# V rows that begin inside the query steps of a PEER stage, with query sums and V sums in different PSUM banks

## The chip, the cores and the metric

The kernel runs on one core of a Trainium2 chip. The metric is the device time of one execution in microseconds (us); less is better. Three runs of the kernel before gave 3059.07 to 3061.05 us, with a median of 3060.49 us.

The core has five engines that run their own instruction queues in order: TensorE (PE in the profile; its weight loads are PEld), VectorE (DVE), ScalarE (ACT), GpSimd (POOL) and SyncE (SP). They wait for each other by semaphores. Transfers between device memory and on-chip memory go over 16 DMA engines; here SP issues the weight loads and POOL issues the gathers.

## The reference

The model is two blocks of layers on 256 tokens of width 2048. The change touches only the last stage, a PEER layer: product keys choose 16 of 16384 experts for each of 8 heads and each token; each chosen expert has a row of `u` and a row of `v`.

```
def peer(x, wq, keys1, keys2, u, v):
    q = (xf @ wq).reshape(t, PEER_HEADS, PEER_QDIM)
    s1 = jnp.einsum('thd,kd->thk', q[..., :half], keys1)
    s2 = jnp.einsum('thd,kd->thk', q[..., half:], keys2)
    ...
    expert = jnp.take_along_axis(cand_i, pos, axis=-1).reshape(t, -1)
    gate = jax.nn.softmax(top_s.astype(jnp.float32), axis=-1)
    ...
        z = jnp.einsum('cd,ced->ce', xc, u[ec])
        act = jax.nn.gelu(z, approximate=False) * gc
        return jnp.einsum('ce,ced->cd', act, v[ec])
```

For each token 8 x 16 rows of `u` are dotted with the token, and 8 x 16 rows of `v` are summed with the weights that come out. Then the result is added to the stream and normalised.

## The kernel before

All tensors of 256 tokens are held as two token tiles of 128 (`TT` = 2). Everything ahead of the last stage is a long list of matmul steps that `run` works through. A step takes one weight tile of 512 KB: `load` brings two such tiles in one transfer of 1 MB, ACT makes a rounded copy `hi` (`split_hi`, L102), DVE the remainder `lo` (`split_lo`, L86), and PE multiplies with both. `run` splits `LOOK_SPLIT` = 3 steps ahead. There are 4 buffers for `lo`, so the split of a step can start only when PE has done the step 4 before it.

The last 32 steps are the queries of the 8 heads: 4 steps a head, built by `unit_B2`, each of 24 matmuls (L417 to L419) that add into one PSUM tile of the head. Here they are called step 0 to step 31, and the heads 0 to 7, so that steps 4h to 4h+3 belong to head h. After a head's fourth step, `e_query` scales the sum (DVE, `eq<-eq,stE_R`, called the query sum's read below), multiplies with the keys (PE, `esc`, L1291), copies the scores (ACT, `es`), and `e_route` finds the 16 experts by a row of small DVE instructions. Head 0 to 7 of token tile 0 are routed first, then those of token tile 1.

A gather (`gather`, L1379, issued by POOL) fetches for each of the 128 tokens of a tile one row of `e_u` or `e_v`: 128 x 2048 x 4 bytes, or 1.049 MB. The text counts these as rows: 256 U rows and 256 V rows, 16 of each for every head and token tile. A U row is worked on by one DVE instruction of 2048 columns (L1410). A V row is worked on by PE: ACT makes a diagonal matrix (`dg`), and four fp32 matmuls of 512 columns (L1428) add the row into `vacc`, which takes 4 PSUM banks; the profile shows 8 matmuls for these. Only some rows of the last two heads are added on DVE.

`e_stream` sets the order of gathers and row work. It is a generator that `run` advances once after every step (`pump`): it issues gathers as long as a row buffer is free, takes the oldest pending row, emits its work, puts the buffer back, and yields. There are 3 row buffers during the query steps. When the last head's scores are copied, `wide_rows` adds 6 more, made of the weight buffers and the token tiles that the queries no longer need; their names begin with `rows_w` and `rows_x`. A V row is allowed (`v_ok`) only after all 8 heads have their scores (`Ee["q"] == EH`) and when its head's U rows are all done; while both kinds are allowed they alternate.

PSUM has two kinds of tiles of two banks each, two of either: `acc_tile` and `side_tile`. Before, a head's query sum takes an `acc_tile`, its scores a `side_tile`, and the V sums of token tile 0 take both `acc_tile`s once the queries are through.

Line numbers are those of the kernel before, unless the text says that they are of the changed kernel (there the V matmuls are L1443, the U instruction L1425, the gather L1394).

Of the kernel before, what the change touches and what calls it, by code (L numbers as in the profile page):

```python
# [22 lines left out]
T = 256  # L23
# [39 lines left out]
def tile_model(ctx: ExitStack, tc: tile.TileContext, x, xT, par, a_in, a_out, kv_in, kv_f, b_in, b_out,  # L63
# [12 lines left out]
    def acc_tile(name):  # L76
        return psum.tile([P, 2, 512], F32, tag="acc", bufs=2, name=name)

    def side_tile(name):
        return psum.tile([P, 2, 512], F32, tag="side", bufs=2, name=name)  # L80

    def w4(name, shape=(P, 1024), dt=F32):
        return work.tile(list(shape), dt, tag="w4", bufs=NW4, name=name)

    def tt_(o, a, b, op):
        V.tensor_tensor(o, a, b, op=op)  # L86

    def mul(o, a, b):
        V.tensor_tensor(o, a, b, op=OP.mult)
# [7 lines left out]
    def stt(o, a, s, b, op0, op1):  # L97
        V.scalar_tensor_tensor(o, a, s, b, op0=op0, op1=op1)  # L98

    def act(o, i, f, bias=0.0, scale=1.0, accum=None):  # L100
        if accum is None:
            S.activation(o, i, f, bias=bias, scale=scale)  # L102
        else:
            S.activation(o, i, f, bias=bias, scale=scale, accum_out=accum)  # L104
# [4 lines left out]
    def spawn(gen):  # L109
        tasks.append(gen)  # L110
# [232 lines left out]
    def resid_norm(st, chunks_ready, xt, wn):  # L343

        for c in range(4):
            while chunks_ready[0] <= c:
                yield
            yield from x_to_T(c, xt, wn)
            norm_chunk(st, c)
        yield  # L350
        yield from norm_end(st)
# [47 lines left out]
        steps[-1].post = lambda: spawn(cb(box["acc"].rearrange("p a (b t) -> p (a b) t", t=T)))  # L399
        return steps  # L400

    def unit_B2(src, xt, cb, name):

        box = {}
        steps = []

        def mm(kt0):
            def f(wh, wl):
                if kt0 == 0:
                    box["acc"] = acc_tile(name)[:, 0, :].rearrange("p (j t) -> p j t", t=T)  # L410
                a = box["acc"]
                h4, l4 = (w_.rearrange("p a (b n) -> p (a b) n", n=T) for w_ in (wh, wl))
                for q in range(4):
                    kt = kt0 + q
                    for j in range(2):
                        w_h, w_l = h4[:, q, j * P:(j + 1) * P], l4[:, q, j * P:(j + 1) * P]
                        PE.matmul(a[:, j, :], lhsT=w_h, rhs=xt.h(kt), start=(kt == 0 and j == 0), stop=False)  # L417
                        PE.matmul(a[:, j, :], lhsT=w_h, rhs=xt.l(kt), start=False, stop=False)
                        PE.matmul(a[:, j, :], lhsT=w_l, rhs=xt.h(kt), start=False, stop=(kt == KT - 1 and j == 1))  # L419
            return f  # L420

        for i in range(4):
            steps.append(Step(src(i // 2), mm(4 * i), ready=lambda k=i: xt.done() > k))
        steps[-1].post = lambda: spawn(cb(box["acc"]))
        return steps
# [269 lines left out]
    steps = []  # L695
# [550 lines left out]
    EH, EK, TK = 8, 128, 16  # L1246
    NG16 = TT * EH
# [2 lines left out]
    stE = Stat("stE")  # L1250
    xtE = Late("xE", "xt0")
    steps[-32].pre = lambda: spawn(resid_norm(stE, xD_done, xtE, "norm_ffn_g_2"))
    Ee = {"q": 0, "route": 0, "nu": 0, "routed": [False] * NG16}
    rows = []

    def e_setup():
# [15 lines left out]
    def gain_rows(t, o):  # L1272
# [2 lines left out]
        mul(o, xs[t], o)  # L1275
        Ee["xw", t] = o

    def e_query(h):

        def f(acc):  # L1280
            while not hasattr(stE, "done"):
                yield
            q = w4(f"eq{h}", (P, 2, T))
            tt_(q, acc, stE.R[:, None, :].to_broadcast([P, 2, T]), OP.mult)
            yield
            if h:
                yield
            ps = side_tile("esc")[:, 0, :].rearrange("p (t k) -> p t k", k=EK)
            for t in range(TT):
                for a_ in range(2):  # L1290
                    PE.matmul(ps[:, t * 2 + a_, :], lhsT=q[:, a_, t * P:(t + 1) * P], rhs=Ee["keys"][:, a_, :],  # L1291
                              start=True, stop=True)
            del q
            if h:
                yield
            if h % 2 == 0:
                Ee["s", h // 2] = w4(f"es{h}", (P, 2, 4, EK))
            s = Ee["s", h // 2][:, h % 2]
            act(s, ps, AF.Copy)
            Ee["q"] += 1  # L1300
            if Ee["q"] == EH:
                wide_rows()
            for t in range(TT):
                while Ee["route"] < t * EH + h or Ee["nu"] < (t * EH + h - 1) * TK - 4:
                    yield
                yield from e_route(h, t, s[:, 2 * t:2 * t + 2, :])
                Ee["route"] += 1
            if h % 2:
                del Ee["s", h // 2]
        return f  # L1310

    def wide_rows():

        for i in range(NRAW):
            rows.append(wpool.tile([P, D], F32, tag="raw", bufs=NRAW, name=f"rows_w{i}"))
        h = acts.tile([P, 2, D], F32, tag="xt0h", name="rows_xh")
        l = acts.tile([P, 2, D], F32, tag="xt0l", name="rows_xl")
        gain_rows(1, h[:, 0, :])
        rows.extend([h[:, 1, :], l[:, 0, :], l[:, 1, :]])
# [58 lines left out]
    def gather(dst, table, gi, k):  # L1378
        G.indirect_dma_start(out=dst, out_offset=None, in_=table, in_offset=bass.IndirectOffsetOnAxis(  # L1379
            ap=Ee["idx"][:, gi, k:k + 1], axis=0))  # L1380

    def e_stream():

        us = [(gi, k) for gi in range(NG16) for k in range(TK)]
        nu = nv = 0
        turn = 0
        pend, accs = [], [None] * TT
        while nv < len(us) or pend:
            while rows:
                v_ok = Ee["q"] == EH and nv < min(nu - nu % TK, len(us)) and \  # L1390
                    (nv // TK < nu // TK - 1 or nu % TK >= 3 or nu == len(us))
                u_ok = nu < len(us) and Ee["routed"][us[nu][0]] and ("xw", us[nu][0] // EH) in Ee
                if v_ok and (turn % 2 or not u_ok):
                    it, nv = ("V",) + us[nv], nv + 1  # L1394
                elif u_ok:
                    it, nu = ("U",) + us[nu], nu + 1
                    Ee["nu"] = nu
                else:
                    break
                turn += 1  # L1400
                r = rows.pop(0)
                gather(r, e_u if it[0] == "U" else e_v, it[1], it[2])
                pend.append((it, r))
            if not pend:
                yield
                continue
            (kind, gi, k), r = pend.pop(0)
            t = gi // EH
            if kind == "U":
                V.scalar_tensor_tensor(r, r, stE.r[:, t:t + 1], Ee["xw", t], op0=OP.mult, op1=OP.mult,  # L1410
                                       accum_out=Ee["z"][:, gi, k:k + 1])
                if k == TK - 1:
                    a_ = Ee["a"][:, gi, :]
                    act(a_, Ee["z"][:, gi, :], AF.Gelu)
                    mul(a_, a_, Ee["gate"][:, gi, :])
            else:
                j = gi % EH * TK + k
                a_ = Ee["a"][:, gi, k:k + 1]
                if gi >= NG16 - 2 and k % 2:
                    stt(xs[t], r, a_, xs[t], OP.mult, OP.add)  # L1420
                else:
                    if j == 0:
                        accs[t] = [(side_tile if t else acc_tile)(f"vacc{t}_{i}") for i in range(2)]
                    dg = Ee["dg"][:, j % 8, :]
                    act(dg, ident, AF.Copy, scale=a_)  # L1425
                    last = j == EH * TK - (2 if t == TT - 1 else 1)
                    for c in range(4):
                        PE.matmul(accs[t][c // 2][:, c % 2, :], lhsT=dg, rhs=r[:, c * 512:(c + 1) * 512],  # L1428
                                  start=(j == 0), stop=last)
                if j == EH * TK - 1:  # L1430
                    spawn(final_tile(t, accs[t]))
            rows.append(r)
            yield

    stF = Stat("stF")
    Fe = {}
# [22 lines left out]

    n0 = len(steps)  # L1460
    for h in range(EH):
        steps.extend(unit_B2(lambda p, h=h: e_q[h, p], xtE, e_query(h), f"eq{h}"))
    steps[n0].pre = lambda: (spawn(e_setup()), spawn(e_stream()))
    run(steps)

# [81 lines left out]
```

## Time and profile before

| what | value |
|---|---|
| median of 3 runs | 3060.49 us |
| the profiled execution's own time | 3060.35 us |
| its span | 3058.6 us |
| PE busy | 2676.6 us (88%) |
| DVE busy | 1928.2 us (63%) |
| ACT busy | 1022.8 us (33%) |
| POOL busy | 774.1 us (25%) |
| moved by DMA | 841.15 MB, mean 275 GB/s |

The span is the time from the first to the last instruction in the trace; the execution's own time has 1.75 us around it. A share of busy time is an average over stages that have different limits. The profile's page cuts the span into 40 slices of 76.5 us, which shows where one stage passes into the next: the last stage's queries lie in the slices from 1663 us on, and the rows are gathered from 1703 us to the end.

### The profile page before, as it was taken

What the parts mean: (1) busy time and instruction counts of PE and PEld (TensorE: products, weight loads), DVE (VectorE), ACT (ScalarE), POOL (GpSimd) and SP (SyncE); (2) the same over time, 40 slices, a digit from 0 to 9 for tenths busy, and PEclk for the clock granted to TensorE, in tenths of its full rate; (3) what the DMA queues carried; (4) which work ended last, traced back from release to release, by engine and by line L of the source; (5) the groups of instructions that cost most, each with busy time, mean ns of one, the idle gap of its engine ahead of it and who ended that gap; (6) DMA issues with size and microseconds to landing.
All of it is one profiled execution on the core that took longest, in us unless ns stands there. A gap on an engine that the chain in (4) does not pass through costs nothing.

```text
span 3058.6 us, 34945 instructions
## 1 busy us (share of the span) xinstructions
PE 2676.6 (88%) x13236; PEld 1959.9 (64%) x13236; DVE 1928.2 (63%) x3020; ACT 1022.8 (33%) x1595; POOL 774.1 (25%) x612
## 2 busy tenths in 40 slices
PE   8999999999999999999999757777777777777766
PEld 8999988888888899999998753223332223322222
DVE  7867665656656558566565896555555665565454
ACT  6545544555554445455455211101111111110000
POOL 0412110000000000000000244554554445444553
PEclk9999999999999999999999879999999999999999
DMA  7444545444444454444455789999999999999997
GB/s 263 146 145 153 178 145 186 168 160 170 168 162 179 174 180 161 171 166 166 179 177 183 270 321 421 421 422 421 421 421 422 421 421 421 421 421 421 422 421 309
DMA packets 118536, 841.15 MB, mean 275 GB/s; under 512 B 13152, under 2 KB 13536, under 8 KB 17376
## 3 DMA queue, kind: packets, MB, share of 16 engines
q0 software_dynamic: 73728, 536.90, 42.4%
q1 hardware_dynamic: 43920, 298.73, 27.3%
q10 hardware_dynamic: 720, 3.28, 0.3%
q8 instruction: 104, 1.70, 0.2%
q14 instruction: 64, 0.52, 0.0%
HBM read 836.77 MB, written 2.10 MB: 274 GB/s over the span
## 4 chain that ended last, share of the span: by engine, by line
PE 59%; DMA 26%; DVE 10%; issue 4%; POOL 1%; ACT 0%; DVEq 0%; POOLq 0%; ACTq 0%
DMA rows_w<-in_e_v_dram,slots 5%; DMA rows_h<-in_e_v_dram,slots 5%; PE vacc L1428 4%; DMA rows_xl<-in_e_v_dram,slots 3%; DMA rows_h<-in_e_u_dram,slots 3%; DMA rows_w<-in_e_u_dram,slots 3%; DMA rows_xl<-in_e_u_dram,slots 2%; DVE rows_h L1410 1%; PE S L579 1%; DMA rows_l<-in_e_v_dram,slots 1%; DMA rows_xh<-in_e_v_dram,slots 1%; DVE eq L86 1%; DVE rows_w L1410 1%; PE aq L391 1%; PE aq L393 1%
## 5 line engine op out<-in xcount | busy, mean ns | idle before, releaser
L86 DVE TENSOR_TENSOR lo<-raw,hi 128x1024 fp32r<-128x1024 f32 x424 | 520.6, 1232 | 297.3 <-PE dx L393 36.3
L102 ACT ACTIVATE hi<-raw 128x1024 fp32r<-128x1024 f32 x424 | 446.7, 1058 | 521.4 <-PE az L392 59.4
L1428 PE MATMUL vacc<-rows_w,dg_ring 128*128 128x512 f32 x640 | 306.0, 623 | 110.5 <-DMA rows_w<-in_e_v_dram,slots 80.2
L1428 PEld LDWEIGHTS vacc<-rows_w,dg_ring 128*128 128x128 f32 x640 | 120.8, 198 | 294.0 <-issue 225.4
L1428 PE MATMUL vacc<-rows_xl,dg_ring 128*128 128x512 f32 x432 | 205.2, 619 | 68.0 <-DMA rows_xl<-in_e_v_dram,slots 55.1
L247 POOL TENSOR_TENSOR rq_y<-rq_m,mhalf 128x8 f32<-128x8 f32 (+2 forms) x24 | 31.6, 1317 | 888.8 <-DVE rq_m L95 882.2
L1428 PE MATMUL vacc<-rows_h,dg_ring 128*128 128x512 f32 x416 | 194.7, 612 | 65.9 <-DMA rows_h<-in_e_v_dram,slots 49.3
L98 DVE SCALAR_TENSOR_TENSOR lo<-raw,prm,hi 128x512 fp32r<-128x512 f32 x256 | 178.8, 748 | 105.0 <-issue 62.0
L102 ACT ACTIVATE hi<-raw,prm 128x512 fp32r<-128x512 f32 x256 | 170.7, 717 | 121.3 <-PE bg L443 31.3
L1428 PEld LDWEIGHTS vacc<-rows_xl,dg_ring 128*128 128x128 f32 x432 | 81.0, 196 | 191.5 <-issue 150.4
L104 ACT ACTIVATE route<-route 128x16 f32<-128x16 f32 x16 | 3.5, 216 | 574.3 <-DVE route L93 574.3
L1428 PEld LDWEIGHTS vacc<-rows_h,dg_ring 128*128 128x128 f32 x416 | 76.9, 193 | 182.6 <-issue 145.1
L1410 DVE SCALAR_TENSOR_TENSOR rows_w<-rows_w,stE_r,rows_xh 128x2048 f32<-128x2048 f32 x42 | 98.7, 2351 | 85.2 <-DMA rows_w<-in_e_u_dram,slots 85.0
L1379 POOL DMA_INDIRECT rows_w<-in_e_u_dram,slots x77 | 116.7, 1516 | 138.8 <-PE vacc L1428 134.8
L1428 PE MATMUL vacc<-rows_l,dg_ring 128*128 128x512 f32 x216 | 104.0, 626 | 46.6 <-DMA rows_l<-in_e_v_dram,slots 40.8
L102 ACT ACTIVATE dg_ring<-ident,slots 128x128 f32<-128x128 f32 x240 | 78.5, 389 | 183.7 <-PE vacc L1428 183.7
L102 ACT ACTIVATE slots<-slots 128x16 f32<-128x16 f32 x16 | 3.4, 216 | 387.8 <-DVE rows_w L1410 139.1
L1428 PE MATMUL vacc<-rows_xh,dg_ring 128*128 128x512 f32 x216 | 103.6, 624 | 33.7 <-DMA rows_xh<-in_e_v_dram,slots 23.8
L1379 POOL DMA_INDIRECT rows_h<-in_e_u_dram,slots x69 | 98.8, 1433 | 134.0 <-PE vacc L1428 85.9
L1410 DVE SCALAR_TENSOR_TENSOR rows_w<-rows_w,stE_r,rows_l 128x2048 f32<-128x2048 f32 x35 | 82.3, 2350 | 66.1 <-DMA rows_w<-in_e_u_dram,slots 66.1
L1410 DVE SCALAR_TENSOR_TENSOR rows_h<-rows_h,stE_r,rows_l 128x2048 f32<-128x2048 f32 x40 | 93.8, 2348 | 43.1 <-DMA rows_h<-in_e_u_dram,slots 43.0
L1428 PEld LDWEIGHTS vacc<-rows_l,dg_ring 128*128 128x128 f32 x216 | 40.9, 199 | 108.8 <-issue 89.6
(482 smaller groups left out, 7450.2 us busy)
## 6 DMA issues: line engine op xcount, KB each, us to landing
raw<-in_d_in_dram SPq DMA_DIRECT2D x76, 1024.0 KB, 4.8
raw<-in_a_in_dram SPq DMA_DIRECT2D x63, 1024.0 KB, 4.7
raw<-in_kv_in_dram SPq DMA_DIRECT2D x32, 1024.0 KB, 4.7
raw<-in_b_in_dram SPq DMA_DIRECT2D x32, 1024.0 KB, 4.8
raw<-in_a_out_dram SPq DMA_DIRECT2D x16, 1024.0 KB, 4.8
raw<-in_b_out_dram SPq DMA_DIRECT2D x16, 1024.0 KB, 4.7
raw<-in_d_out_dram SPq DMA_DIRECT2D x16, 1024.0 KB, 4.8
raw<-in_e_q_dram SPq DMA_DIRECT2D x16, 1024.0 KB, 4.9
```

The lines of the kernel that those rows point to most:

```text
L86: V.tensor_tensor(o, a, b, op=op)
L98: V.scalar_tensor_tensor(o, a, s, b, op0=op0, op1=op1)
L102: S.activation(o, i, f, bias=bias, scale=scale)
L104: S.activation(o, i, f, bias=bias, scale=scale, accum_out=accum)
L247: G.tensor_tensor(y, m, mhalf[:, :w], op=OP.pow)
L391: PE.matmul(a[:, j, :], lhsT=w_h, rhs=xt.h(kt), start=(kt == 0 and j % 2 == 0), stop=False)
L393: PE.matmul(a[:, j, :], lhsT=w_l, rhs=xt.h(kt), start=False, stop=(kt == nk - 1 and j % 2 == 1))
L579: PE.matmul(o, lhsT=lhs[:, h, sl], rhs=r, start=True, stop=True)
L1379: G.indirect_dma_start(out=dst, out_offset=None, in_=table, in_offset=bass.IndirectOffsetOnAxis(ap=Ee["idx"][:, gi, k:k + 1], axis=0))
L1410: V.scalar_tensor_tensor(r, r, stE.r[:, t:t + 1], Ee["xw", t], op0=OP.mult, op1=OP.mult, accum_out=Ee["z"][:, gi, k:k + 1])
L1428: PE.matmul(accs[t][c // 2][:, c % 2, :], lhsT=dg, rhs=r[:, c * 512:(c + 1) * 512], start=(j == 0), stop=last)
```

## The change

`eq_psum` gives the query sums of heads 0 and 1 an `acc_tile` as before. Those of heads 2 to 7 share a single `side_tile`, named `eq_acc`, and take its two banks in turn. The scores of heads 1 to 7 share another `side_tile`, `esc_r`, again bank by bank in turn. So both `acc_tile`s are free after head 1, and the V sums can have them. The condition `Ee["q"] == EH` is taken out of `v_ok`: a V row is allowed as soon as its head's U rows are through. And from the first V row on until the last head has its scores, `e_stream` yields only after every second row, so that a query step carries two.

```
-    def unit_B2(src, xt, cb, name):
+    def unit_B2(src, xt, cb, name, psum_of):
...
-                    box["acc"] = acc_tile(name)[:, 0, :].rearrange("p (j t) -> p j t", t=T)
+                    box["acc"] = psum_of(name).rearrange("p (j t) -> p j t", t=T)
...
-    Ee = {"q": 0, "route": 0, "nu": 0, "routed": [False] * NG16}
+    Ee = {"q": 0, "route": 0, "nu": 0, "beat": 0, "routed": [False] * NG16}
...
+    def eq_psum(h, name):
+
+        if h < 2:
+            return acc_tile(name)
+        if "eq_acc" not in Ee:
+            Ee["eq_acc"] = side_tile("eq_acc")
+        return Ee["eq_acc"]
+
...
-            ps = side_tile("esc")[:, 0, :].rearrange("p (t k) -> p t k", k=EK)
+            if h == 0:
+                assert "eq_acc" not in Ee
+                ps = side_tile("esc")
+            else:
+                if "esc" not in Ee:
+                    Ee["esc"] = side_tile("esc_r")
+                ps = Ee["esc"]
+            ps = ps[:, h % 2, :].rearrange("p (t k) -> p t k", k=EK)
...
-                v_ok = Ee["q"] == EH and nv < min(nu - nu % TK, len(us)) and \
+                v_ok = nv < min(nu - nu % TK, len(us)) and \
                     (nv // TK < nu // TK - 1 or nu % TK >= 3 or nu == len(us))
...
             rows.append(r)
-            yield
+            Ee["beat"] += 1
+            if Ee["q"] == EH or nv == 0 or Ee["beat"] % 2:
+                yield
...
-        steps.extend(unit_B2(lambda p, h=h: e_q[h, p], xtE, e_query(h), f"eq{h}"))
+        steps.extend(unit_B2(lambda p, h=h: e_q[h, p], xtE, e_query(h), f"eq{h}", lambda name, h=h: eq_psum(h, name)[:, h % 2, :]))
```

How the instructions move shows at three places.

**The gathers on POOL, before**, from the 25th U row on. 27 U rows and one V row use the three first buffers (`rows_l`, `rows_h`); the 29th gather is the first into an added one.

```order
L1379 DMA rows_l<-in_e_u_dram,slots 128x2048
L1379 DMA rows_h<-in_e_u_dram,slots 128x2048 x2
L1379 DMA rows_l<-in_e_v_dram,slots 128x2048
L1379 DMA rows_w_16224<-in_e_u_dram,slots 128x2048
L1379 DMA rows_w_16225<-in_e_v_dram,slots 128x2048
L1379 DMA rows_w_16226<-in_e_u_dram,slots 128x2048
```

**The gathers on POOL, changed**: first the 19th to the 23rd gather, then the 33rd to the 37th.

```order
L1394 DMA rows_l<-in_e_u_dram,slots 128x2048
L1394 DMA rows_h<-in_e_v_dram,slots 128x2048
L1394 DMA rows_h<-in_e_u_dram,slots 128x2048
L1394 DMA rows_l<-in_e_v_dram,slots 128x2048
L1394 DMA rows_h<-in_e_u_dram,slots 128x2048
```

```order
L1394 DMA rows_h<-in_e_u_dram,slots 128x2048
L1394 DMA rows_l<-in_e_v_dram,slots 128x2048
L1394 DMA rows_h<-in_e_u_dram,slots 128x2048
L1394 DMA rows_h<-in_e_v_dram,slots 128x2048
L1394 DMA rows_w_16259<-in_e_u_dram,slots 128x2048
```

The 20th gather is now the first V row; from there to the 36th, 9 V rows and 8 U rows alternate in the same three buffers, and the 37th gather is the first into an added one.

**DVE at the query sum's read of head 6, before and changed** (`lo` of step 30, U rows, the read `eq<-...,stE_R`, `lo` of step 31).

```order
L86 TENSOR_TENSOR lo_16066<-raw_15899,hi_16033 128x1024
L1410 SCALAR_TENSOR_TENSOR rows_h,slots<-rows_h,stE_r,rows_l 128x2048
L86 TENSOR_TENSOR eq_16094<-eq_15969,stE_R 128x512
L86 TENSOR_TENSOR lo_16096<-raw_15899,hi_16064 128x1024
L1410 SCALAR_TENSOR_TENSOR rows_l,slots<-rows_l,stE_r 128x2048
```

```order
L86 TENSOR_TENSOR lo_16058<-raw_15893,hi_16025 128x1024
L1425 SCALAR_TENSOR_TENSOR rows_h,slots<-rows_h,stE_r,rows_l 128x2048
L1425 SCALAR_TENSOR_TENSOR rows_l,slots<-rows_l,stE_r 128x2048
L86 TENSOR_TENSOR eq_16088<-eq_acc,stE_R 128x512
L86 TENSOR_TENSOR lo_16090<-raw_15893,hi_16056 128x1024
```

One more U row, the 19th, stands ahead of the read.

**PE where head 7 begins (the end of step 27 and the first matmuls of step 28), before and changed**, with the engines whose semaphores each waits for.

```order
L418 MATMUL eq_15969<-xEl,hi_15931 128x256
L419 MATMUL eq_15969<-xEh,lo_15967 128x256
L417 MATMUL eq_16098<-xEh,hi_15965 128x256 [waits PE_49,Activation_49]
L418 MATMUL eq_16098<-xEl,hi_15965 128x256
L419 MATMUL eq_16098<-xEh,lo_15998 128x256 [waits DVE_49]
```

```order
L418 MATMUL eq_acc<-xEl,hi_15925 128x256
L419 MATMUL eq_acc<-xEh,lo_15961 128x256
L417 MATMUL eq_acc<-xEh,hi_15959 128x256 [waits DVE_49,Activation_49]
L418 MATMUL eq_acc<-xEl,hi_15959 128x256
L419 MATMUL eq_acc<-xEh,lo_15991 128x256
```

The first matmul of the head now waits for DVE, and the third, which needs `lo`, no longer has a wait of its own. The DVE instruction that the new wait counts up to is the read of head 6's query sum out of the same tile `eq_acc`, which stands behind `lo` of step 30 on DVE. It is so at the start of every head from 3 on (steps 12, 16, 20, 24, 28). The V rows then stand on PE between the query steps: one after step 28, one after step 29, one after step 30, three after step 31, and three more behind the `esc` of head 7.

## Rows read from the trace of the kernel before

**Rows 1.** The page, part 2: GB/s moved in each of 40 slices of the span.

```profile
GB/s 263 146 145 153 178 145 186 168 160 170 168 162 179 174 180 161 171 166 166 179 177 183 270 321 421 421 422 421 421 421 422 421 421 421 421 421 421 422 421 309
```

**Rows 2.** Stretches of the last stage: window, then each engine's busy us, granted clock, DMA share, GB/s.

```profile
core 0: us, PE busy (x) PEld busy (x) DVE busy (x) ACT busy (x) POOL busy (x), PEclk, DMA share, GB/s
...
1703.00:1788.00 85.00, 58.90 (x393) 57.59 (x393) 76.03 (x159) 19.27 (x28) 22.33 (x19) 0.80 0.81 300
1788.00:1820.00 32.00, 16.00 (x123) 15.29 (x121) 26.58 (x25) 5.22 (x7) 17.02 (x11) 0.76 0.85 316
1820.00:2960.00 1140.00, 848.51 (x1800) 336.76 (x1800) 668.59 (x1147) 112.09 (x299) 581.13 (x459) 0.97 1.01 421
2960.00:3030.00 70.00, 49.07 (x96) 19.25 (x96) 37.11 (x22) 5.11 (x14) 36.53 (x27) 0.90 1.01 421
```

**Rows 3.** POOL in order of time: start, duration, gather, idle before it and releaser.

```profile
1703.12 1.22 POOL L1379 DMA_INDIRECT rows_l<-in_e_u_dram,slots  x1 [22.73 <-DVE slots L1368]
...
1787.81 0.94 POOL L1379 DMA_INDIRECT rows_l<-in_e_u_dram,slots  x1 [1.73 <-DVE rows_l L1410]
1791.70 1.68 POOL L1379 DMA_INDIRECT rows_h<-in_e_u_dram,slots  x1 [2.95 <-DVE rows_h L1410]
...
1818.31 0.94 POOL L1379 DMA_INDIRECT rows_l<-in_e_v_dram,slots  x1 [0.30 <-DMA rows_xh<-in_f_g_dram]
1819.55 2.31 POOL L1379 DMA_INDIRECT rows_w<-in_e_u_dram,slots  x1 [0.31 <-issue]
```

**Rows 4.** DVE in order of time: reads of query sums, splits and U rows.

```profile
1710.68 2.35 DVE L1410 SCALAR_TENSOR_TENSOR rows_l<-rows_l,stE_r 128x2048 f32<-128x2048 f32 x1 [7.36 <-DMA rows_l<-in_e_u_dram,slots]
...
1741.07 0.69 DVE L86 TENSOR_TENSOR eq<-eq,stE_R 128x512 f32<-128x512 f32 x1
...
1745.42 1.27 DVE L86 TENSOR_TENSOR lo<-raw,hi 128x1024 fp32r<-128x1024 f32 x1
...
1780.05 0.68 DVE L86 TENSOR_TENSOR eq<-eq,stE_R 128x512 f32<-128x512 f32 x1
...
1784.05 1.22 DVE L86 TENSOR_TENSOR lo<-raw,hi 128x1024 fp32r<-128x1024 f32 x1
...
1789.08 2.34 DVE L1410 SCALAR_TENSOR_TENSOR rows_h<-rows_h,stE_r,rows_l 128x2048 f32<-128x2048 f32 x1
...
1792.49 2.34 DVE L1410 SCALAR_TENSOR_TENSOR rows_h<-rows_h,stE_r,rows_l 128x2048 f32<-128x2048 f32 x1
```

**Rows 5.** PE in order of time: two esc groups, two query matmuls, two V rows.

```profile
1694.51 1.06 PE L1291 MATMUL esc<-keys_iota,eq 128*128 128x128 f32 x8
...
1759.85 1.52 PE L1291 MATMUL esc<-keys_iota,eq 128*128 128x128 f32 x8 [3.10 <-DVE eq L86]
...
1791.97 0.28 PE L417 MATMUL eq<-xEh,hi 128*128 128x256 f32 x1
1792.09 0.28 PE L418 MATMUL eq<-xEl,hi 128*128 128x256 f32 x1
...
1827.32 6.08 PE L1428 MATMUL vacc<-rows_l,dg_ring 128*128 128x512 f32 x8 [15.65 <-DMA rows_l<-in_e_v_dram,slots]
...
1846.23 3.60 PE L1428 MATMUL vacc<-rows_xh,dg_ring 128*128 128x512 f32 x8
```

**Rows 6.** Short stretches around a restart of PE, columns as in rows 2.

```profile
1756.00:1760.00 4.00, 0.90 (x8) 0.70 (x7) 3.74 (x17) 1.06 (x1) 0.94 (x1) 1.00 0.97 354
1760.00:1764.00 4.00, 4.00 (x22) 4.00 (x23) 4.00 (x14) 0.00 (x0) 0.53 (x1) 0.57 1.00 369
1764.00:1768.00 4.00, 4.00 (x35) 4.00 (x35) 3.83 (x21) 0.00 (x0) 0.41 (x1) 1.00 1.00 383
```

**Rows 7.** DMA issues from 1703 to 1815 us: count, median us from issue to landing.

```profile
rows_h<-in_e_u_dram,slots POOLq DMA_INDIRECT x17, 7.1
rows_l<-in_e_u_dram,slots POOLq DMA_INDIRECT x9, 6.4
```

## The prediction

> **What bounds the kernel now.** I read the page's slices first, then stretches of the last stage, then POOL, DVE and PE in order of time. The slices show the kernel's two regimes: 145 to 186 GB/s in the weight stages, 421 to 422 from the 25th slice to the 39th [rows 1]. From 1820 us to 3030 us the DMA engines have no gap at 421 GB/s [rows 2]: what counts there is bytes. A row of 1.049 MB takes 2.49 us at that rate. So the time of the kernel is the moment at which this stream begins, plus its bytes, plus a short end. Ahead of it, in the query steps, DMA moves 300 and then 316 GB/s [rows 2], and DVE is busy 76.03 of 85 us: the splits, the routing and the U rows fill it. From 1788 to 1820 us the missing rate is 32 x (1 - 316/421) = 8 us of DMA time. That is what more rows in the query steps could fill at the most.
>
> Three buffers carry the rows until the added ones come. A gather waits on POOL for the row three ahead of it: the 20th stands idle 2.95 us until a U row frees its buffer [rows 3]. The 19th starts at 1787.81 us, the 28th at 1818.31 us [rows 3]: 3.39 us a row, though its transfer is 2.49 us. The first gather into an added buffer is the 29th, at 1819.55 us; from there the stream is full.
>
> **The account.** By the order of gathers the first into an added buffer becomes the 37th, so 8 more rows go ahead of it. The tail behind it loses 8 x 2.49 = 19.9 us. The change in time is therefore the delay of that gather against 1819.55 us, less 19.9 us. Nothing else changes size: the same 512 gathers, DVE and PE instructions, and a tail that is full whichever kind of row comes; both kinds have 9 buffers there, and the last rows on PE and DVE follow the last landing as before. In the tail the V rows lag the U rows by less, which is free at 421 GB/s [rows 2]. A V row's `dg` on ACT is hidden under the gather.
>
> **First term: the wait at the start of each head.** A head's first matmul now waits for the read of the sum before it. The price: PE, which ran two steps ahead, stands still until the read and restarts cold. After 3.10 us of idle time [rows 5] the granted clock is 0.57 in the next 4 us and 1.00 after [rows 6], which is the 1.2 GHz level first and then 2.4 GHz. A step is 24 matmuls at a pitch of 0.12 us [rows 5], 2.9 us at full clock; with its first 4 us at half it takes 4.9 us. The split of a step needs the `lo` buffer of four steps earlier. Step 16 starts after the read at 1741.07 us (0.60 us until the next split), so at 1741.7, and ends at 1746.6; the split of step 20 stood at 1745.42 us [rows 4]: 1.2 us late. Step 20 costs nothing, its follower stands 5 us later. Step 24 starts after the read of 1780.05 us, now 1781.9, and ends at 1786.8; the split of step 28 stood at 1784.05, now 1785.2 [rows 4]: 1.5 us more. Together DVE is 2.7 us late when the V rows begin. The bounds are 0 us (clock stays up: both steps end in time) and about 4 us (both steps at half clock throughout, 5.8 us).
>
> **Second term: 17 gathers in three buffers, with V rows between the query steps.** Costs: a landing 6.9 us after the issue (medians 7.1 and 6.4 [rows 7], weighted by count); a U row 2.3 us on DVE [rows 4]; a V row 3.6 us on PE at full clock, 6.1 us after a long wait [rows 5]; 0.3 us from release to issue; an `esc` 1.1 us. With the 2.7 us:
>
> - The 17th U row ends at 1791.4 + 2.7, so the 20th gather (first V row) issues at 1794.4 and lands at 1801.3. The 18th U row stood at 1792.49 [rows 4], now 1795.2; the 19th follows and ends at 1799.8, and only then comes the read of head 6.
> - Step 28 waits for that read, until 1800.4. PE has been idle since 1796.5, so the step takes 4.9 us, to 1805.3. The first V row, landed for 4 us, stands behind it on PE: 1805.3 to 1809.0. Only now its buffer is free: the 23rd gather at 1809.3.
> - Step 29 to 1811.9, second V row to 1815.5, `esc` and step 30 to 1819.5, third V row to 1823.2. Its successor, gather 27, issues at 1823.5, lands at 1830.4; that U row ends at 1832.7; gather 30 at 1833.0 lands at 1839.9.
> - That is the sixth V row. The fifth was done at 1836, so PE has idled 4 us and this one takes 6.1 us, to 1846.0. Gather 33 at 1846.3 lands at 1853.2, the U row ends at 1855.5, gather 36 goes at 1855.8 and gather 37 1.2 us behind it, at **1857.0 us**.
>
> The delay is 1857.0 - 1819.55 = 37.5 us; less 19.9 us this leaves **17.6 us slower**. The profiled execution took 3060.35 us of its own, 0.14 us under the median of the runs; 3060.35 + 17.6 is **3078 us**.
>
> Bounds: if PE keeps its full clock, the first term is gone (2.7 us), step 28 saves 2.0 and the sixth V row 2.5 us, and with landings of 6.4 us the three on the chain save 1.5: 8.9 us slower, 3069 us. Upwards: landings of 7.6 us (the first gather: issue 1703.12 [rows 3], U row 1710.68 [rows 4]) add 2 us, and two further V rows at half clock 5 us: 24.6 us, 3085 us. I take the middle because the idle times of 4 us that the chain gives are longer than the 3.10 us after which the rows show half clock.
>
> The Trainium skill (Perfetto Trace Analysis, Optimizing Tensor Performance, Matmuls) asks that independent matmul groups rotate through PSUM banks, so that the reading of one overlaps the next. By that the first term would be nothing, since the query sums do rotate; the built program waits all the same, by tile and not by bank, and I go by the wait. The rival below on that wait says what the time would be.
>
> **Rivals.**
>
> The wait at the head's start is hidden (the bank rotation works as meant). Then step 28 ends at 1792.0 as before (step 29 begins at 1791.97 [rows 5]); the first V row lands at 1798.6, cold until 1804.7; steps and V rows follow to 1818.9, gather 27 at 1819.2, gather 30 at 1828.7, sixth V row cold to 1841.7, gather 36 at 1851.5, gather 37 at 1852.7: 33.2 - 19.9 = 13 us slower, 3074 us. For it: the banks differ. Against: the wait stands in the order of PE.
>
> PE takes the V rows in its gaps and only the buffers' turn counts, at the 3.39 us that they showed with U rows alone [rows 3]: gather 37 at 1791.70 + 16 x 3.39 + 1.24 = 1847.2, 27.6 - 19.9 = 7.7 us slower, 3068 us. For it: PE is busy only 16.00 of 32 us there [rows 2]. Against: the first V row's place is behind step 28.
>
> Faster: the V rows need no DVE, which is the busy engine, so they fill the DMA gaps, and the three buffers turn at the 2.49 us of a transfer. Gather 37 at 1791.70 + 16 x 2.49 + 1.24 = 1832.8; 13.2 - 19.9 = 6.7 us faster, 3054 us. It decides at 2.91 us a row, where the delay is just 19.9 us. For it: DVE is what held the buffers. Against: landing, row work and issue alone are 6.9 + 0.3 + (2.3 + 3.6)/2 = 10.2 us for three buffers, 3.4 us a row. The same page (Optimization Strategy) says that a kernel with several regimes may gain by interleaving them, which is this rival; no row here shows it for three buffers.
>
> The change does not do what it says, V rows come no earlier: 3060 us. The order of gathers speaks against it.
>
> **How the numbers follow.** The chain with its bounds, 3069 to 3085 us, has 0.62, and the hidden wait, inside the same range, 0.10. The buffers' turn alone (3068) has 0.11, a heavier chain above 3085 us 0.07, the faster case 0.07, no effect 0.03. The measurement tells 0.2%, some 6.1 us, from no change: above 3066.6 is slower, below 3054.4 faster. Of the case at 3068 I put 0.03 within that bound. So slower has 0.62 + 0.10 + 0.08 + 0.07 = 0.87, the same 0.03 + 0.03 = 0.06, faster 0.07. The range 3063 to 3085 leaves out the faster case, no effect and the heavier chain: 0.17.
>
> **What would show it.** In the profile after: the 37th gather, the first into `rows_w`, at about 1857 us (1833 if the faster rival holds, 1847 for the turn alone); step 28 beginning after the read of head 6 with several us of idle time that DVE ends; the first V row starting straight behind step 28, long after its landing; gathers 20 to 36 some 3.8 us apart; DMA at 421 GB/s from some 1860 us on, and a rate under 316 GB/s between 1795 and 1855 us. It is wrong if PE is not late at step 28, or if the 17 gathers stand under 2.91 us apart.

## The result and the profile after

| kernel | median | lowest to highest |
|---|---|---|
| before | 3059.92 us | 3059.05 to 3061.05, 6 runs |
| changed | 3080.97 us | 3078.57 to 3083.17, 6 runs |

The ratio is 1.0067, with a 95% interval of 1.0056 to 1.0078: the change makes the kernel slower by 21 us. The profiled execution took 3083.17 us, the longest of the six and 2.2 us over the median, with a span of 3081.4 us; before it was 3058.6 us, so the spans differ by 22.8 us. About 1.8 us of that is scatter between executions, which the moments read from this trace may carry with them.

The slices of the page, 77.0 us wide here and 76.5 us before, show where:

```profile
GB/s 261 151 144 157 165 164 179 164 159 169 164 164 189 172 168 171 159 177 160 183 175 182 287 259 388 421 421 421 422 422 421 421 422 422 421 419 421 422 422 309
```

Against [rows 1], the 24th slice has 259 GB/s instead of 321, and the 25th 388 instead of 421. From the 26th on the stream is as full as before. The same in stretches of the last stage, with the columns of [rows 2] (the last two short ones are for the section on the hardware):

```profile
1703.00:1788.00 85.00, 49.93 (x344) 49.44 (x345) 72.86 (x154) 17.97 (x25) 21.13 (x18) 0.76 0.81 299
1788.00:1820.00 32.00, 27.61 (x168) 23.33 (x167) 18.56 (x18) 7.01 (x14) 11.46 (x8) 0.89 0.60 224
...
1820.00:1866.00 46.00, 31.68 (x84) 14.98 (x83) 18.20 (x29) 2.46 (x4) 17.75 (x14) 0.85 0.79 291
1866.00:2984.00 1118.00, 831.66 (x1753) 329.56 (x1752) 658.22 (x1123) 110.34 (x295) 571.01 (x448) 0.96 1.01 421
...
1834.00:1840.00 6.00, 5.37 (x8) 2.01 (x8) 1.40 (x2) 0.00 (x0) 2.00 (x3) 0.72 0.74 265
1844.00:1848.00 4.00, 3.51 (x15) 1.88 (x13) 1.07 (x1) 0.46 (x1) 0.94 (x1) 1.00 0.93 373
```

In the kernel before, 1820 to 1866 us read

```profile
1820.00:1866.00 46.00, 32.45 (x62) 13.78 (x63) 32.19 (x72) 7.51 (x19) 30.02 (x22) 0.76 1.01 420
```

These rows nearly close the account in bytes. Before, the three stretches moved 0.300 x 85 + 0.316 x 32 + 0.420 x 46 = 54.9 MB; now they move 0.299 x 85 + 0.224 x 32 + 0.291 x 46 = 46.0 MB. The 8.9 MB that are missing cost 8.9 / 0.421 = 21 us at the rate of the stream, of 22.8 us. The query steps up to 1788 us move what they did. All of the loss lies between 1788 and 1866 us, where the rows of both kinds turn in three buffers. DVE, the busy engine before (26.58 of 32 us), is down to 18.56 us there: it waits for rows.

PE in order of time, with the columns of [rows 5]: the starts of heads 4, 6 and 7 (steps 16, 24 and 28), and the first seven V rows.

```profile
1741.60 0.55 PE L417 MATMUL eq_acc<-xEh,hi 128*128 128x256 f32 x1 [9.61 <-DVE eq L86]
...
1782.05 0.55 PE L417 MATMUL eq_acc<-xEh,hi 128*128 128x256 f32 x1 [6.04 <-DVE eq L86]
...
1801.13 0.55 PE L417 MATMUL eq_acc<-xEh,hi 128*128 128x256 f32 x1 [4.39 <-DVE eq L86]
...
1806.39 4.01 PE L1443 MATMUL vacc<-rows_h,dg_ring 128*128 128x512 f32 x8
...
1813.10 3.60 PE L1443 MATMUL vacc<-rows_l,dg_ring 128*128 128x512 f32 x8
1820.30 3.60 PE L1443 MATMUL vacc<-rows_h,dg_ring 128*128 128x512 f32 x8
1827.80 3.67 PE L1443 MATMUL vacc<-rows_h,dg_ring 128*128 128x512 f32 x8 [1.03 <-DMA rows_h<-in_e_v_dram,slots]
1834.02 5.37 PE L1443 MATMUL vacc<-rows_l,dg_ring 128*128 128x512 f32 x8 [2.55 <-DMA rows_l<-in_e_v_dram,slots]
1842.94 3.67 PE L1443 MATMUL vacc<-rows_h,dg_ring 128*128 128x512 f32 x8 [3.56 <-DMA rows_h<-in_e_v_dram,slots]
1850.66 5.37 PE L1443 MATMUL vacc<-rows_h,dg_ring 128*128 128x512 f32 x8 [3.15 <-DMA rows_h<-in_e_v_dram,slots]
```

Each of these heads starts behind several us of idle time that ends with DVE's read of the query sum, as `eq L86` at the end of the rows says; so do heads 3 and 5, at 1717.37 and 1761.11 us. The first V row stands straight behind step 28. The first three V rows have no bracket: their data had landed, and they only had their turn on PE behind a query step. From the fourth on it is the other way round: PE waits for each of these rows to land. POOL in order of time, with the columns of [rows 3] (the 20th, 23rd, 27th, 30th, 33rd, 36th and 37th gather):

```profile
1794.97 1.68 POOL L1394 DMA_INDIRECT rows_h<-in_e_v_dram,slots  x1 [2.95 <-DVE rows_h L1425]
...
1810.67 0.94 POOL L1394 DMA_INDIRECT rows_h<-in_e_u_dram,slots  x1 [7.75 <-PE vacc L1443]
...
1824.17 0.94 POOL L1394 DMA_INDIRECT rows_h<-in_e_u_dram,slots  x1 [3.47 <-PE vacc L1443]
...
1835.03 0.93 POOL L1394 DMA_INDIRECT rows_h<-in_e_v_dram,slots  x1 [0.30 <-issue]
...
1846.89 0.94 POOL L1394 DMA_INDIRECT rows_h<-in_e_u_dram,slots  x1 [3.36 <-PE vacc L1443]
...
1860.20 2.75 POOL L1394 DMA_INDIRECT rows_h<-in_e_v_dram,slots  x1 [2.97 <-DVE rows_h L1425]
1863.25 0.94 POOL L1394 DMA_INDIRECT rows_w<-in_e_u_dram,slots  x1 [0.30 <-issue]
```

Gathers wait for PE now, where they waited for DVE in [rows 3]. From the 20th to the 36th they come (1860.20 - 1794.97) / 16 = 4.08 us apart, and the first into an added buffer starts at 1863.25 us. The waits from 1788 to 1864 us (engine, line, releaser: us in total, times, longest) put the two sides of this turn together:

```profile
DVE rows_h L1425 <- DMA rows_h<-in_e_u_dram,slots: 24.7, 4, 8.4
POOL rows_h L1394 <- PE vacc L1443: 24.4, 5, 7.7
...
POOL rows_l L1394 <- PE vacc L1443: 7.8, 2, 4.1
```

POOL waits 24.4 + 7.8 us for V rows to free a buffer, and DVE 24.7 us for U rows to land, most of which could only be asked for after such a wait.

### The profile page after: what moved, and what is told of

It is laid out like the page before. It is cut to its first block, busy times and chain, and to the rows that moved or that the text cites. A ratio compares the mean times of both kernels' runs of the same rounds, so it can differ in the third digit from the quotient of the medians.

```text
span 3081.4 us, 34936 instructions
## 1 busy us (share of the span) xinstructions
PE 2689.7 (87%) x13236; PEld 1964.3 (64%) x13236; DVE 1928.9 (63%) x3020; ACT 1022.8 (33%) x1595; POOL 775.5 (25%) x612
## 4 chain that ended last, share of the span: by engine, by line
PE 59%; DMA 25%; DVE 9%; issue 5%; POOL 2%; ACT 0%; POOLq 0%; DVEq 0%; ACTq 0%
DMA rows_w<-in_e_v_dram,slots 7%; PE vacc L1443 4%; DMA rows_h<-in_e_v_dram,slots 4%; DMA rows_h<-in_e_u_dram,slots 3%; DMA rows_xl<-in_e_u_dram,slots 2%; DMA rows_w<-in_e_u_dram,slots 2%; DMA rows_l<-in_e_v_dram,slots 2%; DMA rows_xl<-in_e_v_dram,slots 2%; DMA rows_l<-in_e_u_dram,slots 1%; DVE rows_h L1425 1%; PE S L579 1%; DMA rows_xh<-in_e_v_dram,slots 1%; DVE eq L86 1%; PE aq L391 1%; PE aq L393 1%
## 5 line engine op out<-in xcount | busy, mean ns | idle before, releaser
L86 DVE TENSOR_TENSOR lo<-raw,hi 128x1024 fp32r<-128x1024 f32 x424 | 520.6, 1232 | 300.4 <-PE dx L393 36.3
L1443 PE MATMUL vacc<-rows_w,dg_ring 128*128 128x512 f32 x616 | 294.3, 623 | 104.8 <-DMA rows_w<-in_e_v_dram,slots 75.1
L1443 PE MATMUL vacc<-rows_h,dg_ring 128*128 128x512 f32 x456 | 222.4, 633 | 72.6 <-DMA rows_h<-in_e_v_dram,slots 56.6
L1443 PE MATMUL vacc<-rows_xl,dg_ring 128*128 128x512 f32 x408 | 192.8, 617 | 63.7 <-DMA rows_xl<-in_e_v_dram,slots 49.3
L1443 PEld LDWEIGHTS vacc<-rows_h,dg_ring 128*128 128x128 f32 x456 | 87.4, 201 | 203.1 <-issue 165.3
L1443 PE MATMUL vacc<-rows_l,dg_ring 128*128 128x512 f32 x232 | 117.3, 653 | 43.9 <-DMA rows_l<-in_e_v_dram,slots 36.3
```

## The experiments

My theory had two parts. The first is a wait at each head's start: the query sums of heads 2 to 7 lie in different banks of one tile, and the program waits by tile. The second is that three buffers cannot carry 17 rows of both kinds with V rows in line on PE. The rivals: either part alone makes the loss; or V rows between query steps are bad in themselves, with whatever buffers; or a transfer that moved with them is what costs.

**The shared tiles alone.** V rows wait for the last query again; only the PSUM arrangement of the change is left, since its yield after every second row comes into play only while V rows begin early.

```
-                v_ok = nv < min(nu - nu % TK, len(us)) and \
+                v_ok = Ee["q"] == EH and nv < min(nu - nu % TK, len(us)) and \
```

> The change's two shared tiles alone: query sums of heads 2 to 7 in one tile, scores of heads 1 to 7 in another, but V rows begin as before, only when all heads have their scores, and one row goes with a step. Theory (the wait per tile at the start of each head makes PE restart cold and holds back the splits): DVE late by about 3 us at the split of step 28 and the last heads later still, so 3 to 6 us slower than before, some 3063 to 3066 us, with the first gather into an added buffer at about 1823 us. Rival (the shared tile costs nothing as long as no V row stands behind it): within 1 us of before, 3059 to 3061 us.

Measured: 3063.93 us (3062.93 to 3066.5), ratio 1.0015 (1.0006 to 1.0024), so 4.5 us over the 3059.41 us of the kernel before, measured beside it. PE waits at the start of step 24 and again, for a shorter time, of step 28:

```profile
1780.96 0.55 PE L417 MATMUL eq_acc<-xEh,hi 128*128 128x256 f32 x1 [6.26 <-DVE eq L86]
...
1797.54 0.36 PE L417 MATMUL eq_acc<-xEh,hi 128*128 128x256 f32 x1 [2.11 <-DVE eq L86]
```

The first gather into an added buffer, still the 29th, starts at 1823.32 us, 3.8 us after that of [rows 3]. So the wait costs by itself, though it hides no V row: banks of one tile don't separate the heads.

**Two tiles in turn.** From head 2 on, even heads take one tile and odd heads another; in each the query sum has bank 0 and the scores bank 1. V rows come early as in the change.

```
+    def pair(h):
+        if ("pair", h % 2) not in Ee:
+            Ee["pair", h % 2] = side_tile(f"pair{h % 2}")
+        return Ee["pair", h % 2]
...
+            ps = pair(h or 1)[:, 1, :].rearrange("p (t k) -> p t k", k=EK)
```

> The change, but each side tile serves the heads of one parity: its first bank the query sum, its second the scores. So a head's first matmul no longer waits for the read of the head before; V rows and two rows a step stay. Theory (the wait costs some 7 us, the rest is the turn of three buffers with V rows queued on PE): the 37th gather some 5 to 7 us earlier than in the change, 3073 to 3077 us. Rival A (the wait is the whole loss): about 3060 us. Rival B (the wait is hidden): about 3081 us.

Measured: 3073.67 us (3071.03 to 3074.84), ratio 1.0043 (1.0030 to 1.0057): 7.3 us better than the change, still 14.3 us over the 3059.41 us of the kernel before, measured beside it. The first V row and the 37th gather:

```profile
1796.90 3.67 PE L1440 MATMUL vacc<-rows_h,dg_ring 128*128 128x512 f32 x8 [2.54 <-DMA rows_h<-in_e_v_dram,slots]
```

```profile
1854.45 0.94 POOL L1391 DMA_INDIRECT rows_w<-in_e_u_dram,slots  x1 [0.31 <-issue]
```

PE is ahead now and waits for the row, not the row for PE; yet the 20th to the 36th gather, from 1790.61 to 1851.40 us, still come 3.80 us apart. The 37th gather is 8.8 us earlier than in the change, more than the 5 to 7 us expected, though the time lies inside its forecast.

The wait for DVE's read is gone at both steps: step 28 now follows step 27 without idle time. A tile shared by a query sum and scores still makes a wait of its own. At the start of step 24 PE stands idle for 9.16 us, until ACT has copied the scores of head 4 out of the same tile:

```profile
1776.19 0.58 PE L417 MATMUL pair<-xEh,hi 128*128 128x256 f32 x1 [9.16 <-ACT es L102]
```

It ends 5.9 us before that of the change (1782.05 us) and holds no gather back: the 19th and the 20th come 1.1 us earlier than in [rows 3], at 1786.73 and 1790.61 us, as the first does by 1.0 us. The Trainium skill (Perfetto Trace Analysis, Optimizing Tensor Performance, Matmuls) asks for independent groups to rotate through PSUM banks. The two experiments agree with its aim, and show that here it takes tiles: with banks rotating inside one tile the query steps waited for DVE's read (6.26 and 2.11 us at steps 24 and 28), and with two tiles they did not.

**One row a query step.** A plain `yield` after each row, so fewer V rows lie ahead of the added buffers.

```
-            Ee["beat"] += 1
-            if Ee["q"] == EH or nv == 0 or Ee["beat"] % 2:
-                yield
+            yield
```

> The change, but a query step carries one row, as before; V rows still begin early and the tiles are shared. The first gather into an added buffer is then the 29th again, and three V rows instead of nine stand before it. Theory (each row that is put through the three buffers ahead of the added ones loses some 1.3 us against the full stream, and V rows hold the query steps on PE): about half of the loss goes, 3067 to 3073 us. Rival (V rows early are the loss, however many): 3078 us or more. Rival (only the two rows a step lose, the rest gains): under 3060 us.

Measured: 3069.25 us (3068.27 to 3069.54), ratio 1.0030 (1.0019 to 1.0042). The first gather into an added buffer is the 29th again, at 1828.51 us: 9.0 us late, and the time is 9.8 us over. Fewer rows through three buffers cost less, about half of the change's loss; but no order that was run gains while the buffers are three (one row a step with two tiles was not run with three).

**Three added buffers early.** The change, with the three weight buffers handed to the rows one by one at steps 24, 26 and 28, when the last weights no longer need them.

```
+    for i in range(NRAW):
+        steps[n0 + 24 + 2 * i].pre = lambda i=i: rows.append(
+            wpool.tile([P, D], F32, tag="raw", bufs=NRAW, name=f"rows_w{i}"))
```

> The change, but the three weight buffers join the row buffers as soon as their last weight tile is split (from steps 24, 26 and 28 on) instead of after the last head's scores. Order of rows on PE and DVE nearly as in the change. Theory (the turn of three buffers sets the pace of gathers 20 to 36): the gathers run ahead of the row work and the stream has its bytes in flight while PE works through the queries; most of the loss goes, 3061 to 3068 us. Rival (PE's order, the cold clock and the wait per tile are the loss, buffers do not matter): 3077 us or more.

Measured: 3063.15 us (3061.66 to 3064.45), ratio 1.0010 (1.0001 to 1.0019), 17.8 us better than the change, with V rows in the same places between the query steps and the wait at the head's start still there. Its row for the stretch of the loss:

```profile
1788.00:1820.00 32.00, 27.58 (x167) 23.30 (x167) 20.91 (x20) 7.04 (x14) 14.15 (x10) 0.89 0.90 329
```

PE works as much as in the change (27.58 and 27.61 us), while DMA moves 329 instead of 224 GB/s. So the V rows on PE are not in themselves what costs; that the gathers have to wait for them is. Not all of the 17.8 us belongs to the change, though: the next experiment shows that the same buffers gain 6.7 us without it, so 11.1 us of its loss goes with them.

**The same early buffers without the change.**

> The kernel before, but the three weight buffers join the row buffers from steps 24, 26 and 28 on; no V row begins early, tiles as before. Theory (buffers, not the kind of row, leave DMA idle from 1788 to 1820 us): gathers run up to three rows ahead, which takes up to 7.5 us of transfers out of the tail; the idle DMA time there was 8 us: 3053 to 3057 us. Rival (DVE is what limits the rows there, so more buffers only wait longer): 3059 to 3061 us.

Measured: 3053.25 us (3052.66 to 3054.27) against 3059.92 us, ratio 0.9977 (0.9968 to 0.9986): 6.7 us faster than the kernel before.

```profile
1788.00:1820.00 32.00, 14.94 (x120) 14.44 (x118) 31.52 (x68) 3.62 (x5) 18.78 (x11) 0.77 1.00 409
```

U rows alone fill the DMA engines, at 409 instead of 316 GB/s [rows 2], and DVE has time for them: 31.52 us of 32. The 8 us of missing DMA time that the prediction read there were a lack of buffers and not of V rows. A sentence of the Trainium skill (Perfetto Trace Analysis, Optimization Strategy) fits this row: consistent bubbles can mean that there isn't enough SBUF or PSUM for the next tile.

**Two tiles in turn and early buffers**, with V rows early as in the change: the edits of the second and the fourth experiment together.

> The change with the tiles by parity of the head (no wait at the head's start) and with the weight buffers as row buffers from steps 24, 26 and 28 on. Theory (three causes: wait per tile, turn of three buffers, V rows queued on PE between query steps; the first two are taken out, and V rows need no DVE): the stream is nearly full from about 1790 us, 3051 to 3057 us, faster than before. Rival (V rows on PE delay the queries so much that the early start cannot pay): 3058 us or more.

Measured: 3052.86 us (3051.35 to 3054.83), ratio 0.9977 (0.9967 to 0.9987). It beats both kernels of this document, and stands level with the early buffers alone, 0.4 us apart.

```profile
1788.00:1820.00 32.00, 31.30 (x166) 22.27 (x166) 21.05 (x19) 3.67 (x9) 18.22 (x13) 1.00 1.00 402
```

The six medians, in us, lay the parts side by side (beside the runs of 3073.67 and 3063.15 us the kernel before came to 3059.41 us, beside the others to 3059.92 us, so differences are good to half a us at best):

| | three buffers | three more, early |
|---|---|---|
| V rows after the queries (before) | 3059.92 | 3053.25 |
| V rows early, two banks of a tile (the change) | 3080.97 | 3063.15 |
| V rows early, two tiles | 3073.67 | 3052.86 |

Read down, V rows early without the wait cost 13.8 us with three buffers and nothing (-0.4) with six. The wait costs 7.3 us with three and 10.3 us with six. So 11.1 of the change's 21 us go with the buffers, and what is left then, 9.9 us against the early buffers alone, is the wait.

**That kernel with one row a step.**

> As the run with both mended causes, but one row a query step. Theory: with six buffers the gathers are ahead in either case, so this equals the run with two rows a step within 2 us. Rival (two rows a step are what fills the stream): 3 us or more above it. Rival (V rows on PE cost by number): 3 us or more below it.

Measured: 3055.38 us (3054.2 to 3057.7), ratio 0.9986 (0.9977 to 0.9995), 2.5 us above the kernel with two rows a step, measured beside it, and so between the two cases expected (within 2 us, or 3 us and more); DMA moves 375 instead of 402 GB/s from 1788 to 1820 us. Two rows a step seem to be worth a little once buffers are there; with three buffers they cost 11.7 us (3080.97 against 3069.25 us).

**The gain-row transfer of token tile 1 left out**, once from the change and once from the kernel before. The gain of token tile 1 is not computed in these two: DVE copies the token tile (1.22 us) where it multiplied it with the gain (2.29 us).

```
+        if t:
+            ts(o, xs[t], 1.0, OP.mult)
+        else:
+            nc.scalar.dma_start(o, f_g[1:2, :].to_broadcast([P, D]))
+            mul(o, xs[t], o)
```

The reason is a wait that the prediction did not have. The 33rd gather is issued at 1846.89 us, and its U row, with the columns of [rows 4], starts only at 1857.57 us:

```profile
1857.57 2.35 DVE L1425 SCALAR_TENSOR_TENSOR rows_h<-rows_h,stE_r,rows_l 128x2048 f32<-128x2048 f32 x1 [8.29 <-DMA rows_h<-in_e_u_dram,slots]
```

That is 10.7 us, where the kernel before has 7.1 as a median [rows 7]. At 1847.55 us, between this gather and its landing, ACT issues 1 MB of gain rows. The DMA issues from 1845 to 1860 us of the change (KB each, median us to landing):

```profile
rows_xh<-in_f_g_dram ACTq DMA_DIRECT2D x1, 1024.0 KB, 10.1
rows_h<-in_e_u_dram,slots POOLq DMA_INDIRECT x2, 9.3
rows_l<-in_e_v_dram,slots POOLq DMA_INDIRECT x1, 10.4
```

> The change without the transfer of 1 MB that brings the gain row for token tile 1 behind head 7's scores (rows of that tile are then not multiplied with the gain: a part of the computation is left out). In the change this transfer is in flight with gather 33, which took 10.7 us to its U row where the forecast had 6.9. Theory (the transfer shares the DMA engines with the last gather of the chain and holds the first gather into an added buffer back by its own 2.5 us or more): gather 37 some 2.5 to 4 us earlier, 3077 to 3078.5 us. Rival (gather 33 is late for another reason): within 1 us of the change, 3080 to 3082 us.

Measured: 3077.04 us (3075.66 to 3079.67), ratio 1.0055 (1.0041 to 1.0069), 3.9 us better than the change. The 33rd gather goes at 1847.08 us, and its U row follows 6.5 us later:

```profile
1853.55 2.35 DVE L1428 SCALAR_TENSOR_TENSOR rows_h<-rows_h,stE_r,rows_l 128x2048 f32<-128x2048 f32 x1 [3.71 <-DMA rows_h<-in_e_u_dram,slots]
```

The 37th gather comes 3.8 us earlier, at 1859.41 us, so the whole of it reaches the end. It is made of two parts, though. The 36th gather is 2.0 us earlier, at 1858.16 us: its buffer is free sooner, but POOL first has to issue the 35th, which waits for a V row on PE until 1856.58 us. The other 1.8 us is the issue of the 36th gather itself, which took 0.94 us here and 2.75 us in the change. There it began at 1860.20 us, while DVE was at the multiplication with the gain:

```profile
1859.85 2.29 DVE L89 TENSOR_TENSOR rows_xh<-xs,rows_xh 128x2048 f32<-128x2048 f32 x1
```

This ended at 1862.14 us, and the issue 0.81 us later; the last section shows how regular that is. So the edit took out two things, the transfer beside the 33rd gather and the multiplication beside the 36th, and only the moments of the traces tell them apart; no run has one without the other.

> The kernel before without the same transfer (the gain is left out for token tile 1). It says what the transfer costs where it meets a nearly full stream: at most its 2.5 us of bytes, 3057 to 3059.5 us. If the change gains more than this by the same edit, the surplus is the chain's.

Measured: 3060.0 us (3057.36 to 3061.22) against 3059.76 us, ratio 0.9998 (0.9989 to 1.0007). The saving that was expected, at most 2.5 us, did not come. In the kernel before the same transfer and multiplication cost nothing that can be told, though the transfer, issued at 1811.71 us, has the same neighbour there: the gather issued at 1812.08 us took 9.9 us to its U row.

```profile
1821.94 2.35 DVE L1410 SCALAR_TENSOR_TENSOR rows_h<-rows_h,stE_r,rows_l 128x2048 f32<-128x2048 f32 x1 [0.89 <-DMA rows_h<-in_e_u_dram,slots]
```

By then the first gather into an added buffer had already been issued, at 1819.55 us [rows 3]. The 3.9 us are the price of the gain rows' new place on the chain.

## Why the prediction was right, and where its sizes were off

The forecast was 3078 us, the median came to 3080.97 us, inside the range, with slower as the likeliest case. Its chain is the one that the trace shows, moment by moment:

| moment | predicted | measured |
|---|---|---|
| split of step 28 (DVE) | 1786.8 | 1787.32 |
| first matmul of step 28 (PE) | 1800.4 | 1801.13 |
| 27th gather (POOL) | 1823.5 | 1824.17 |
| 30th gather | 1833.0 | 1835.03 |
| 33rd gather | 1846.3 | 1846.89 |
| 36th gather | 1855.8 | 1860.20 |
| 37th gather, first into `rows_w` | 1857.0 | 1863.25 |

**The account** held. From the first gather into an added buffer to the end of the span it was 3058.6 - 1819.55 = 1239.1 us, and is 3081.4 - 1863.25 = 1218.2 us: 20.9 us less, where the prediction took 19.9. The delay is 43.7 us instead of 37.5; the scatter of the profiled execution, some 1.8 us, may be part of it.

**The first term**, the wait at the head's start, was right in kind and a little small. The split of step 28 is 3.3 us later than in [rows 4], in a run whose first gather starts 0.4 us earlier (1702.73 us): 3.7 us instead of 2.7, inside the bounds of 0 and 4. Alone it costs 4.5 us of the median (shared tiles alone), and within the change 7.3 us (two tiles), since step 28 with the first V row behind it waits as well. The sum had that, as the way from 1792.0 to 1805.3 us, but I had put the rival without the wait at 3074 us, 4 us below the forecast; the measured kernel for it, at 3073.67 us, bears out the rival's size (its 37th gather came at 1854.45 us where the rival had 1852.7), and the distance is larger because the forecast was low.

**The second term**, 17 gathers in three buffers, is the larger part of the loss, as predicted: without the wait the early V rows cost 13.8 us with three buffers and nothing with six. It was mis-sized in its last links. Against the forecast the lag of the chain is 0.7 us at the 27th gather, 2.0 at the 30th (its buffer's U row began 7.4 us after the 27th gather, not 6.9, and the 29th gather, issued beside that U row, kept POOL until 1834.72 us, 0.8 us too long), 0.6 at the 33rd, 4.4 at the 36th and 6.25 at the 37th. Three sizes failed:

- "a landing 6.9 us after the issue" for the 33rd gather: 10.7 us, 3.8 us more. The step that failed is "Nothing else changes size": the gain rows' transfer moves too, from beside U rows to beside this gather. Without it the landing is 6.5 us, and the 36th gather comes 2.0 us earlier.
- "gather 37 1.2 us behind it": the 36th gather held POOL for 2.75 us, beside the gain rows' multiplication on DVE, so it took 3.05 us, 1.85 more. The sum had every issue at its short length.
- "this one takes 6.1 us" for the sixth V row, after an idle time of 4 us: it took 3.67 us, after 3.56 us. This 2.4 us in the other direction hid a part of the rest: the lag falls from 2.0 to 0.6 us there, although the landing ahead of it was 1.0 us too long. That the forecast came within 3 us of the median is in part luck.

**The range** reached 3085 us by landings 0.7 us longer each and by V rows at half clock. The landings did lengthen, but unevenly, one by 3.8 us, and that by another cause.

**The rivals.** "Only the buffers' turn counts", 3.39 us a row, fell with 4.08 us measured, and 3.80 us without the wait. "Faster" wanted under 2.91 us a row. Its idea, that V rows fill DMA gaps because they need no DVE, is not wrong: it works with six buffers, and then gives no more than U rows do. Of the Trainium skill's rule on kernels with several regimes (Perfetto Trace Analysis, Optimization Strategy: interleaving them may help) these runs show the condition: interleaved, the kernel lost 13.8 us with three buffers and gained 7.1 us with six, the gain coming from the buffers.

What stays open: what the transfer and the multiplication of the gain rows cost one by one, and why two rows a step are 2.5 us better than one with six buffers. Neither was tried.

## What to carry to other kernels

Before work of another kind is moved into a gap of the DMA engines, count what carries it: with three buffers at 3.39 us a row the gap was made by the buffers, and rows that hold a buffer until their turn on PE made it wider; three buffers a little earlier brought more than any order. Independent sums on PE want tiles of their own where the program waits by tile; a bank of the same tile isn't enough. And of a stage that shifts in time every transfer and every instruction beside it counts, also those that were free where they stood.

## What was not expected of the hardware

A gather's landing depends on what flies with it: 6.5 us from issue to the U row's start without the gain transfer beside it, 10.7 us with it, although each of these transfers is about 1 MB. The kernel before shows the same beside its gain transfer, 9.9 us. In the same stretch a V row's gather took 10.4 us and the gain transfer itself 10.1 us.

A gather's issue on POOL seems to be held up by DVE. From 1700 to 1880 us of the change POOL issues 45 gathers; 27 take about 0.94 us and 18 take 1.2 to 3.0 us. Of these 18 all but the first end 0.81 us after the end of a DVE instruction that was running when they began, as the 36th does (DVE until 1862.14 us, POOL until 1862.95 us). In the kernel before it is 23 of 24 in the same stretch. That DVE is the cause is read from these moments; no run took such an instruction away by itself.

How long PE had been idle does not by itself tell the clock of the next V row. After 2.55, 3.15 and 4.04 us of idle time V rows took 5.37, 5.37 and 6.24 us, and the stretch around the first of these has a granted clock of 0.72, a mean of the two levels, 1.2 and 2.4 GHz. After 3.56 us the sixth took 3.67 us, and its stretch from 1844 us shows 1.00, the upper level throughout. What PE did ahead of it was the V row at 1834.02 us and that idle time; what made the difference was not tried.
